# Four plain up-projections at the start of the ConvFFN, its quarter sums made in steps beside them, and the down-projection of a pair one product later

## The chip, the cores and the metric

The kernel runs on one NeuronCore of a Trainium2 chip. The metric is the device time of one execution in microseconds. The engines have the profile's names: PE is the tensor engine (PEld its weight loads), DVE the vector engine (VectorE in the text), ACT the scalar engine (ScalarE), POOL is GpSimd, and SP issues most of the DMAs.

## The reference

A trunk of two layers, d = 1024, over 1024 prompt tokens and 8 x 4 sampled tokens. Each layer is a mixer (RWKV-7, GLA and RetNet heads side by side, then `w_out`), a layer norm, a gated convolutional FFN and another layer norm. The change lies in the FFN alone:

```python
def _conv_ffn(x, conv0, w_up, conv_w, conv_b, w_down):
    t_ = x.shape[1]
    u = x @ w_up                                   # (tokens, 1024) @ (1024, 2 * 2816)
    buf = jnp.concatenate([conv0.astype(u.dtype), u], axis=1)
    c = conv_b + sum(conv_w[j] * buf[:, j:j + t_] for j in range(CONV_W))   # 3 taps over time
    a, b = jnp.split(c, 2, axis=-1)
    return (jax.nn.gelu(a) * b) @ w_down, buf[:, -(CONV_W - 1):]

f, cv = _conv_ffn(x, s_conv[l], ffn_up[l], ffn_conv_w[l], ffn_conv_b[l], ffn_down[l])
x = _layer_norm(ALPHA * x + f, ln2_g[l], ln2_b[l])
```

## The kernel before, in words

Features lie on the 128 partitions, tokens along the free axis in three blocks n = 0, 1, 2 of 384, 384 and 288 columns (`NB`; the last holds the sampled tokens). A matrix product in f32 accuracy is done with operands split into a high and a low half (`split`: ScalarE casts the high half, GpSimd or VectorE subtracts it for the low half), three matmuls for each 128 x 128 weight tile (`mm3`). So x1, the FFN's input, exists as x1h and x1l, eight row tiles (m or k = 0 to 7) for each n; a weight piece of 128 x 512 arrives raw (tag wr, five buffers, `FR`) and becomes wh and wl (six buffers each, `FW`).

The 2816 hidden features are 22 tiles (`NJ`). Tile j has a first half (feature tile j, through the GELU) and a gate half (feature tile j + 22); the two together are called block j here. The blocks are worked in pairs: after the up-projections of a pair come its convolution, gating (`up_gate`, which leaves the gated tile as hh and hl) and, one pair later, its down-projection.

*Plain blocks* (`up_blocks`, blocks 0 and 1): for each n and each of the two feature tiles, two products of 4 k-tiles (12 matmuls each) into a PSUM bank (pu), then bank to u, convolution in c, gating.

*Winograd blocks* (`up`, blocks 2 to 21): for n = 0 and 1 the 2 x 2 block product (two feature tiles or halves of k against two token blocks) is done with seven products instead of eight (pa, pg, pb, pc, pf, pd, pe in the profile). They take sums of weight pieces (s1, s2, s3, s4, made on VectorE from the raw pieces r11, r12, r21, r22) and sums of quarters of x1 (t2, t3, t4, and one that replaces a quarter of x1h and x1l), made once a layer by `sums`. Block n = 2 stays plain beside it (p in the profile), four half products of 12 matmuls with 288 columns.

*The sums before.* At the start of block 1, `residual` adds x1h and x1l into acc for n = 0 and 1 (16 GpSimd instructions a layer). After n = 1 of block 1, `sums` makes the quarter sums from acc, four VectorE instructions for each of four k, each followed by a split.

*The down-projection* (`downs`, `down`): for two halves of the output tiles, two weight pieces (wD) of the pair's two blocks, and for each n and four tiles six matmuls into a bank pd (five buffers, shared with the products), which VectorE adds into acc. `up` of the pair's even block calls it through `between`. The engines' order is set by the framework's scheduler, which knows the order of the code and what each instruction waits for; TensorE follows the code. A tile's buffer is reused when all instructions on the old tile are done.

Of the kernel before, what the change touches and what calls it, by code (L numbers as in the profile page):

```python
# [10 lines left out]
F32 = mybir.dt.float32  # L11
# [158 lines left out]
def step_kernel(ctx: ExitStack, tc: tile.TileContext, xT, wA, wB, wO, wU, wD, pp, pb, lora, bg, bgk, shT, cvT, srw, sgl, srt,  # L170
# [150 lines left out]
    for l in range(depth):  # L321
# [1090 lines left out]
        def wu(t, half):  # L1412
            return wU[l, t, :, 4 * half:4 * half + 4]
# [4 lines left out]
        def whole(ap, name):  # L1418
            return piece(raw_piece(ap, name), name)
# [52 lines left out]

        def residual():

            for k in range(4):
                for n, m in ((0, k), (1, k), (1, k + 4), (0, k + 4)):
                    G.tensor_tensor(acc[n][m], x1[n][0][:, m].bitcast(F32), x1[n][1][:, m].bitcast(F32), ALU.add)

        def sums():


            (h0, l0, _), (h1, l1, _) = x1[:2]
            t2, t3, t4 = ([jp.tile([P, 4, 384], F32R, tag="tq", name=f"{n}{p}", bufs=6) for p in "hl"] for n in ("t2", "t3", "t4"))

            def two(h, lo, raw, e):
                A.copy(h, raw)
                e.tensor_tensor(lo, raw, h.bitcast(F32), ALU.subtract)
            for k in range(4):
                r11, r12, r21, r22 = acc[0][k], acc[1][k], acc[0][k + 4], acc[1][k + 4]
                d1, d2, d3, d4 = (fp.tile([P, 386], F32, tag="u", name="d", bufs=6)[:, 0:384] for _ in range(4))  # L1490
                V.tensor_tensor(d3, r22, r12, ALU.subtract)
                V.tensor_tensor(d1, r12, r11, ALU.subtract)
                V.tensor_tensor(d2, r22, d1, ALU.subtract)
                V.tensor_tensor(d4, r21, d2, ALU.subtract)
                for h, lo, d, e in ((t2[0][:, k], t2[1][:, k], d2, V), (h1[:, k], l1[:, k], d1, V),
                                    (t3[0][:, k], t3[1][:, k], d3, G), (t4[0][:, k], t4[1][:, k], d4, G)):
                    two(h, lo, d, e)
            return [(h0[:, 0:4], l0[:, 0:4]), (h0[:, 4:8], l0[:, 4:8]), (h1[:, 4:8], l1[:, 4:8]), (h1[:, 0:4], l1[:, 0:4]), t2, t3, t4]

# [7 lines left out]

        def up_blocks(j):

            w = [[whole(wu(j + i * NJ, half), f"wU{j}") for half in range(2)] for i in range(2)]  # L1510
            prev, hs, qs = [None] * 2, [], None
            if j:
                residual()
            for n in range(3):
                cs = []
                for i in range(2):
                    t = j + i * NJ
                    ps = bank(n, f"pu{t}")
                    for half in range(2):
                        hf = slice(4 * half, 4 * half + 4)  # L1520
                        product(ps, w[i][half], (x1[n][0][:, hf], x1[n][1][:, hf]), half == 0, half == 1)
                    if n < 2:
                        u = new_u()
                        halo(u, n, prev[i])
                        A.copy(u[:, 2:386], ps)
                        c = conv_prompt(t, i, u, ps, n == 0)
                    else:
                        c, u = conv_samples(t, i, ps)
                        conv_rest(t, c, u, prev[i])
                    prev[i] = u  # L1530
                    cs.append(c)
                hs.append(up_gate(cs, n))
                if n == 0 and j == 0:
                    stats3[0]()
                if n == 1 and j:
                    qs = sums()
            return hs, qs

        def up(j, qs, late=False, between=lambda: None):
# [23 lines left out]
            c11 = conv_prompt(t0, 0, u11, v11, True)  # L1563
            between()
            if not late:
# [10 lines left out]
            v12 = u12[:, 2:386]  # L1576
            V.tensor_tensor(v12, v22, pb_, ALU.add)
            p5 = bank(0, "pc")
            product(p5, piece(s1, "s1"), q1)
# [40 lines left out]
        def down(m, n, group, hs, ws):  # L1620
            ps = pd.tile([P, 512], F32, tag="d", name="pd")[:, :NB[n][1]]
            for i, (h, w) in enumerate(zip(hs, ws)):
                mm3(ps, *w, *h[n], i == 0, i == len(hs) - 1)
            a = acc[n][m]
            if n == 2 and group < 2:

                if group:
                    V.tensor_tensor(a, a, ps, ALU.add)
                V.scalar_tensor_tensor(a, x1[n][group][:, m].bitcast(F32), ALPHA, a if group else ps, ALU.mult, ALU.add)
            elif group:  # L1630
                V.tensor_tensor(a, a, ps, ALU.add)  # L1631
            else:
                V.scalar_tensor_tensor(a, a, ALPHA, ps, ALU.mult, ALU.add)

# [6 lines left out]

        hs, qs = [None] * 2, None
        for j in range(2):
            hs[j], qs = up_blocks(j)
        for j in range(2, NJ - 2, 2):

            a = up(j, qs, between=lambda: downs(j - 2, hs, j // 2 - 1))
            hs = [a, up(j + 1, qs)]

# [215 lines left out]
```

## Time and profile before

| | us |
|---|---|
| median of three runs | 3475.77 (3475.0 to 3477.01) |
| profiled execution | 3467.65 |
| its span, first to last instruction | 3465.5 |
| TensorE busy in it | 3128.6 |
| FFN of the first layer, first to last up-projection pair | about 879 to 1660 from the start |
| FFN of the second layer | about 2616 to 3440 |

In the rows of the profile, a line number is one of the kernel before; L140 stands for all matmuls and L197 for all splits, so the tile names tell them apart. A row of a timeline is start, duration, engine, line, operation, output and inputs, shapes, and in brackets the idle time before it and what ended it. A row of a list of waits is who waited for whom, total us, times, longest. A row of busy time by stretches is start:end and length, busy time and instructions of PE, PEld, DVE, ACT and POOL, the granted clock of TensorE, the DMA share and GB/s.

### The profile page before, as it was taken

The numbers are of one execution on the slowest core, as the hardware profiler recorded it, in microseconds if no ns is written. First come the engines' busy times: TensorE is split into PE (matmuls) and PEld (weight loads), VectorE is DVE, ScalarE is ACT, GpSimd is POOL, SyncE is SP. The second block draws the span as 40 slices with busy tenths as digits, with TensorE's granted clock in tenths as the row PEclk, the third lists the DMA queues.
The fourth block names the chain that finished last, engine by engine and source line by source line (L and its number), as shares of the span: only waits on it lengthen the run. The fifth ranks groups of instructions, "written<-read, shape, count | busy, mean of one in ns | idle before, by whom it ended". The sixth has DMA issues, their size and how long they took to land. (4 is left out here: it accounts for less than half of the span.)

```text
span 3465.5 us, 59055 instructions
## 1 busy us (share of the span) xinstructions
PE 3128.6 (90%) x21570; PEld 2880.9 (83%) x21570; DVE 2382.5 (69%) x5061; ACT 1592.4 (46%) x3639; POOL 1593.6 (46%) x1524
## 2 busy tenths in 40 slices
PE   8889999998799999999788899998987899999995
PEld 8778887778789999999687788876777899998995
DVE  3587764666778776767857667644667786767678
ACT  6653432645443343334585533335555433433346
POOL 5542322145654554545675322121446554555456
PEclk9989999988999999999899899998989999999997
DMA  7443224343211111111364332233432111111111
GB/s 247 144 119 84 75 62 131 113 139 107 52 43 46 43 49 46 40 46 53 97 196 141 107 82 71 64 127 97 140 106 58 46 46 40 49 46 43 44 51 67
DMA packets 245566, 291.14 MB, mean 84 GB/s; under 512 B 76620, under 2 KB 158316, under 8 KB 245276
## 3 DMA queue, kind: packets, MB, share of 16 engines
q1 hardware_dynamic: 225004, 274.08, 25.9%
q10 hardware_dynamic: 20272, 13.29, 1.5%
q8 instruction: 170, 2.79, 0.3%
q14 instruction: 120, 0.98, 0.1%
HBM read 228.85 MB, written 58.43 MB: 83 GB/s over the span
## 5 line engine op out<-in xcount | busy, mean ns | idle before, releaser
L1433 DVE SCALAR_TENSOR_TENSOR c<-u,ppt,c 128x32 f32<-128x32 f32 (+3 forms) x704 | 496.5, 740 | 128.6 <-ACT c L1437 124.3
L197 POOL TENSOR_TENSOR wil<-wir,wih 128x512 fp32r<-128x512 f32 (+1 forms) x264 | 369.0, 1408 | 252.2 <-ACT wih L197 230.1
L140 PE MATMUL gt<-wih,xh 128*128 128x320 f32 (+1 forms) x1008 | 346.4, 345 | 4.6 <-DVE mx L404 4.6
L140 PE MATMUL gt<-wil,xh 128*128 128x320 f32 (+1 forms) x1008 | 321.2, 320 | 4.6 <-POOL wil L197 4.6
L1631 DVE TENSOR_TENSOR acc<-acc,pd 128x384 f32<-128x384 f32 (+1 forms) x464 | 230.7, 516 | 99.3 <-PE pd L140 99.1
L140 PE MATMUL gt<-wih,xl 128*128 128x320 f32 x896 | 285.3, 318 | 0.0
L197 ACT CAST wih<-wir 128x512 fp32r<-128x512 f32 (+1 forms) x296 | 185.1, 637 | 138.7 <-PE po L140 61.9
L140 PE MATMUL pa<-xh,wih 128*128 128x384 f32 (+1 forms) x576 | 208.1, 361 | 29.1 <-ACT wih L197 11.3
L653 DVE TENSOR_TENSOR tm<-U,N 96x60 f32<-96x60 f32 (+24 forms) x558 | 173.3, 310 | 78.0 <-DMA N<-gd 62.9
L140 PEld LDWEIGHTS gt<-wih,xh 128*128 128x128 f32 (+1 forms) x1008 | 191.7, 190 | 42.0 <-issue 24.5
L140 PE MATMUL pa<-xh,wil 128*128 128x384 f32 (+1 forms) x576 | 196.4, 341 | 12.9 <-POOL wil L197 11.6
L140 PEld LDWEIGHTS gt<-wil,xh 128*128 128x128 f32 (+1 forms) x1008 | 192.9, 191 | 8.4 <-POOL wil L197 6.9
L140 PE MATMUL pa<-xl,wih 128*128 128x384 f32 (+1 forms) x576 | 195.1, 339 | 1.2 <-POOL xl L197 1.2
L655 DVE TENSOR_TENSOR U<-U,tm 96x60 f32<-96x60 f32 (+24 forms) x558 | 170.1, 305 | 16.3 <-DMA ydram<-ys 0.4
L140 PEld LDWEIGHTS gt<-wih,xl 128*128 128x128 f32 x896 | 176.2, 197 | 0.0
L197 POOL TENSOR_TENSOR hl<-c,hh 128x384 fp32r<-128x384 f32 x132 | 147.3, 1127 | 55.6 <-ACT hh L197 55.6
L140 PEld LDWEIGHTS pa<-xh,wih 128*128 128x128 f32 x576 | 116.6, 202 | 43.6 <-ACT wih L197 12.6
L1437 ACT ACTIVATE c<-u,ppt 128x384 f32<-128x384 f32 x160 | 113.1, 708 | 74.2 <-POOL hl L197 38.2
L140 PE MATMUL po<-yh,wih 128*128 128x384 f32 (+1 forms) x384 | 138.5, 361 | 8.6 <-DVE ac L1349 7.6
L140 PE MATMUL po<-yh,wil 128*128 128x384 f32 (+1 forms) x384 | 130.6, 340 | 2.2 <-DVE wil L197 2.2
L140 PEld LDWEIGHTS pa<-xh,wil 128*128 128x128 f32 x576 | 116.5, 202 | 17.3 <-POOL wil L197 15.8
L140 PE MATMUL po<-yl,wih 128*128 128x384 f32 (+1 forms) x384 | 130.4, 339 | 0.0
(958 smaller groups left out, 10257.4 us busy)
## 6 DMA issues: line engine op xcount, KB each, us to landing
wir<-in_wA_dram SPq DMA_DIRECT2D x144, 256.0 KB
wir<-in_wO_dram SPq DMA_DIRECT2D x96, 256.0 KB
wir<-in_wB_dram SPq DMA_DIRECT2D x56, 320.0 KB
tokd<-ev SPq DMA_DIRECT2D x112, 160.0 KB
x<-rkvd SPq DMA_DIRECT2D x16, 576.0 KB
tk<-tokd SPq DMA_DIRECT2D x16, 480.0 KB
rkvd<-mx SPq DMA_DIRECT2D x36, 192.0 KB
tk<-tokd SPq DMA_DIRECT2D x16, 400.0 KB
```

The costliest lines, as they stand in the source:

```text
L140: self.order(self.engine.matmul(out, lhsT, rhs, start=start, stop=stop), cols, 4 if rhs.dtype == F32 else 1)
L197: return A.copy(dst_h, src), (le or G).tensor_tensor(dst_l, src, dst_h.bitcast(F32), ALU.subtract)
L653: V.tensor_tensor(tm, U[:, 0:nr, i:i + 1].to_broadcast([4 * ns, nr, 31 - i]), N[:, i:i + 1, i + 1:32].to_broadcast([4 * ns, nr, 31 - i]), ...
L655: V.tensor_tensor(U[:, 0:nr, i + 1:32], U[:, 0:nr, i + 1:32], tm, ALU.add)
L1433: V.scalar_tensor_tensor(cv[..., o:], uu[..., tap + o:tap + w], pc(PP_CV + 4 * t + tap), cv[..., o:], ALU.mult, ALU.add)
L1437: A.activation(c, src, AF.Identity, scale=pc(PP_CV + 4 * t + 2), bias=pc(PP_CV + 4 * t + 3))
L1631: V.tensor_tensor(a, a, ps, ALU.add)
```

## The change

Blocks 2 and 3 become plain too (`up_first` for block 0, `up_plain` for blocks 1 to 3, which work through one feature tile and its three n before the other). `residual` is gone: the accumulation of the first pair adds x1h and x1l itself, in two VectorE instructions for every tile. `sums` becomes a generator in five steps, called by `then` after given points of blocks 1 to 3, and works from x1h and x1l instead of acc; the last step replaces the quarter of x1. In a Winograd block `between` stands behind the sum of product pb instead of in front of the second half product of n = 2.

```diff
-        def residual():
-
-            for k in range(4):
-                for n, m in ((0, k), (1, k), (1, k + 4), (0, k + 4)):
-                    G.tensor_tensor(acc[n][m], x1[n][0][:, m].bitcast(F32), x1[n][1][:, m].bitcast(F32), ALU.add)
...
+            def apart(e, a, b):
+
+                d, f = new(), new()
+                e.tensor_tensor(d, a[0], b[0], ALU.subtract)
+                e.tensor_tensor(f, a[1], b[1], ALU.subtract)
+                e.tensor_tensor(d, d, f, ALU.add)
+                return d
+
+            def minus(e, a, d):
+
+                e.tensor_tensor(d, a[0], d, ALU.subtract)
+                e.tensor_tensor(d, d, a[1], ALU.add)
             for k in range(4):
-                r11, r12, r21, r22 = acc[0][k], acc[1][k], acc[0][k + 4], acc[1][k + 4]
...
-                V.tensor_tensor(d3, r22, r12, ALU.subtract)
-                V.tensor_tensor(d1, r12, r11, ALU.subtract)
-                V.tensor_tensor(d2, r22, d1, ALU.subtract)
-                V.tensor_tensor(d4, r21, d2, ALU.subtract)
...
+                d = apart(G, x(1, k + 4), x(1, k))
+                two(t3[0][:, k], t3[1][:, k], d, G)
+                d = apart(V, x(1, k), x(0, k))
+                minus(V, x(1, k + 4), d)
+                two(t2[0][:, k], t2[1][:, k], d, G)
+                f = new()
+                V.tensor_tensor(f, x(0, k + 4)[0], d, ALU.subtract)
+                V.tensor_tensor(f, f, x(0, k + 4)[1], ALU.add)
+                two(t4[0][:, k], t4[1][:, k], f, V)
+                yield
+            for k in range(4):
+                d = apart(V if k % 2 else G, x(1, k), x(0, k))
+                two(h1[:, k], l1[:, k], d, V)
+            yield
...
+        def up_plain(j, between, then):
+
+            hs, cs = [], []
+            for i in range(2):
+                t = j + i * NJ
+                w, prev = [whole(wu(t, half), f"wU{t}") for half in range(2)], None
+                for n in range(3):
+                    c, prev = plain(t, i, n, w, prev)
+                    cs.append(c)
+                    if i:
+                        hs.append(up_gate((cs[n], c), n))
+                    then(j, i, n)
+                if i == 0:
+                    between()
+            return hs
...
             c11 = conv_prompt(t0, 0, u11, v11, True)
-            between()
             if not late:
                 product(p1, piece(r21, "a21"), x2[0], True, False)
...
             V.tensor_tensor(v12, v22, pb_, ALU.add)
+            between()
             p5 = bank(0, "pc")
...
-            if n == 2 and group < 2:
-
-                if group:
-                    V.tensor_tensor(a, a, ps, ALU.add)
-                V.scalar_tensor_tensor(a, x1[n][group][:, m].bitcast(F32), ALPHA, a if group else ps, ALU.mult, ALU.add)
-            elif group:
+            if group:
                 V.tensor_tensor(a, a, ps, ALU.add)
             else:
-                V.scalar_tensor_tensor(a, a, ALPHA, ps, ALU.mult, ALU.add)
+
+                for x, y in zip(x1[n][:2], (ps, a)):
+                    V.scalar_tensor_tensor(a, x[:, m].bitcast(F32), ALPHA, y, ALU.mult, ALU.add)
...
-        hs, qs = [None] * 2, None
-        for j in range(2):
-            hs[j], qs = up_blocks(j)
-        for j in range(2, NJ - 2, 2):
-
-            a = up(j, qs, between=lambda: downs(j - 2, hs, j // 2 - 1))
-            hs = [a, up(j + 1, qs)]
+
+        make = sums()
+        qs = next(make)
+        times = ((1, 0, 2), (1, 1, 2), (2, 0, 2), (2, 1, 2), (3, 1, 1))
+
+        def then(*at):
+            if at in times:
+                next(make)
+        hs = []
+        for j in range(0, NJ - 2, 2):
+
+            def between():
+                if j:
+                    downs(j - 2, hs, j // 2 - 1)
+            if j == 0:
+                a = up_first()
+            elif j < 4:
+                a = up_plain(j, between, then)
+            else:
+                a = up(j, qs, between=between)
+            hs = [a, up(j + 1, qs) if j >= 4 else up_plain(j + 1, lambda: None, then)]
```

Where instructions stand now. First GpSimd around the down-projection of blocks 4 and 5 (wD4, wD5), which stands in block 6 (its weights are wU6 and wU28, its splits a21 and s2; hl are the low halves of the gated tiles of block 5). Before:

```order
L197 TENSOR_TENSOR wD4wl<-wD4r,wD4wh 128x512
L197 TENSOR_TENSOR wD5wl<-wD5r,wD5wh 128x512
L1454 COPY cvt<-u 128x16
L1453 COPY cvt<-u 128x2
L197 TENSOR_TENSOR wD4wl<-wD4r,wD4wh 128x512
L197 TENSOR_TENSOR hl<-c,hh 128x384
L197 TENSOR_TENSOR wD5wl<-wD5r,wD5wh 128x512
L197 TENSOR_TENSOR a21wl<-wU28r,a21wh 128x512
L1454 COPY cvt<-u 128x16
L1453 COPY cvt<-u 128x2
L197 TENSOR_TENSOR hl<-c,hh 128x384
L197 TENSOR_TENSOR hl<-c,hh 128x288
```

The same place in the changed kernel:

```order
L197 TENSOR_TENSOR a21wl<-wU28r,a21wh 128x512
L197 TENSOR_TENSOR s2wl<-wU6r,s2wh 128x512
L1454 COPY cvt<-u 128x16
L1453 COPY cvt<-u 128x2
L197 TENSOR_TENSOR wD4wl<-wD4r,wD4wh 128x512
L197 TENSOR_TENSOR hl<-c,hh 128x384
L197 TENSOR_TENSOR wD5wl<-wD5r,wD5wh 128x512
L1454 COPY cvt<-u 128x16
L1453 COPY cvt<-u 128x2
L197 TENSOR_TENSOR hl<-c,hh 128x288
L197 TENSOR_TENSOR hl<-c,hh 128x384
L197 TENSOR_TENSOR wD4wl<-wD4r,wD4wh 128x512
```

The splits of a21 and s2 moved ahead of all wD splits; the gated tiles' halves stand behind the first two wD splits instead of four, and that of n = 2 comes before that of n = 1.

VectorE's sums of weights for block 6 (s1, then wU28 for r21, wU6 for r11 and r12). Before, they stand beside the first accumulations of the down-projection, behind the sum of pg:

```order
L1569 TENSOR_TENSOR s1r<-wU28r 128x512
L1433 SCALAR_TENSOR_TENSOR c<-u,ppt,c 128x32
L1562 TENSOR_TENSOR u<-u,pg 128x384
L1433 SCALAR_TENSOR_TENSOR c<-u,ppt,c 128x32
L1570 TENSOR_TENSOR wU28r<-wU6r,wU28r 128x512
L1631 TENSOR_TENSOR acc_10128<-acc_10128,pd 128x384
L1571 TENSOR_TENSOR wU6r<-s1r,wU6r 128x512
L1433 SCALAR_TENSOR_TENSOR c<-u,ppt,c 128x383
L1631 TENSOR_TENSOR acc_10129<-acc_10129,pd 128x384
L1572 TENSOR_TENSOR wU6r<-wU6r 128x512
```

In the changed kernel, they stand between the sums of products pb, pf, pc and pd of block 5:

```order
L1602 TENSOR_TENSOR s1r<-wU28r 128x512
L1610 TENSOR_TENSOR u<-u,pb 128x384
L1603 TENSOR_TENSOR wU28r<-wU6r,wU28r 128x512
L1616 TENSOR_TENSOR u<-u,pf 128x384
L1604 TENSOR_TENSOR wU6r<-s1r,wU6r 128x512
L1617 TENSOR_TENSOR u<-u,pc 128x384
L1605 TENSOR_TENSOR wU6r<-wU6r 128x512
L1623 TENSOR_TENSOR u<-u,pd 128x384
```

They moved forward by about a block's second half, past the convolution and gating of block 5.

GpSimd at block 1 (wU1 are its weights; acc the residual sums). Before, these rows are the end of a run of 15 sums between two weight splits:

```order
L1477 TENSOR_TENSOR acc_10131<-x1h_9172,x1l_9173 128x384
L1477 TENSOR_TENSOR acc_10139<-x1h_9682,x1l_9683 128x384
L1477 TENSOR_TENSOR acc_10143<-x1h_9682,x1l_9683 128x384
L197 TENSOR_TENSOR wU1wl<-wU1r,wU1wh 128x512
L1477 TENSOR_TENSOR acc_10135<-x1h_9172,x1l_9173 128x384
```

In the changed kernel (d are the temporaries of the quarter sums):

```order
L197 TENSOR_TENSOR wU23wl<-wU23r,wU23wh 128x512 x2
L1453 COPY cvt<-u 128x2
L197 TENSOR_TENSOR wU2wl<-wU2r,wU2wh 128x512 x2
L1454 COPY cvt<-u 128x16 x2
L1453 COPY cvt<-u 128x2
L197 TENSOR_TENSOR hl<-c,hh 128x384
L1495 TENSOR_TENSOR d<-x1h_9682 128x384
L1496 TENSOR_TENSOR d<-x1l_9683 128x384
```

No sum stands ahead of a split of block 1's weights any more.

More of the change, by code (lines that the diff above doesn't have):

```diff
@@ L1483, in sums, with x, new @@
             t2, t3, t4 = ([jp.tile([P, 4, 384], F32R, tag="tq", name=f"{n}{p}", bufs=6) for p in "hl"] for n in ("t2", "t3", "t4"))
+            def x(n, k):
+                return [t[:, k].bitcast(F32) for t in x1[n][:2]]
+            qs = [(h0[:, 0:4], l0[:, 0:4]), (h0[:, 4:8], l0[:, 4:8]), (h1[:, 4:8], l1[:, 4:8]), (h1[:, 0:4], l1[:, 0:4]), t2, t3, t4]
+            yield qs
+            def new():
+                return fp.tile([P, 386], F32, tag="u", name="d", bufs=6)[:, 0:384]
             def two(h, lo, raw, e):
@@ L1487, in two @@
                 e.tensor_tensor(lo, raw, h.bitcast(F32), ALU.subtract)
-            for k in range(4):
-                r11, r12, r21, r22 = acc[0][k], acc[1][k], acc[0][k + 4], acc[1][k + 4]
-                d1, d2, d3, d4 = (fp.tile([P, 386], F32, tag="u", name="d", bufs=6)[:, 0:384] for _ in range(4))
-                V.tensor_tensor(d3, r22, r12, ALU.subtract)
-                V.tensor_tensor(d1, r12, r11, ALU.subtract)
-                V.tensor_tensor(d2, r22, d1, ALU.subtract)
-                V.tensor_tensor(d4, r21, d2, ALU.subtract)
[L1495 to L1498, printed above, removed]
+            def apart(e, a, b):
[7 more added lines that the diff above has]
+                e.tensor_tensor(d, d, a[1], ALU.add)
+            for k in range(4):
+                d = apart(G, x(1, k + 4), x(1, k))
[12 more added lines that the diff above has]
+            yield
         def product(ps, w, x, first=True, last=True):
@@ L1506, in bank, with plain, up_first @@
             return (pg.tile([P, 512], F32, tag="g", name=name) if n == 2 else pd.tile([P, 512], F32, tag="d", name=name))[:, :NB[n][1]]
[L1508 to L1513, printed above, removed]
+        def plain(t, i, n, w, prev):
+            ps = bank(n, f"pu{t}")
+            for half in range(2):
+                hf = slice(4 * half, 4 * half + 4)
+                product(ps, w[half], (x1[n][0][:, hf], x1[n][1][:, hf]), half == 0, half == 1)
+            if n < 2:
+                u = new_u()
+                halo(u, n, prev)
+                A.copy(u[:, 2:386], ps)
+                return conv_prompt(t, i, u, ps, n == 0), u
+            c, u = conv_samples(t, i, ps)
+            conv_rest(t, c, u, prev)
+            return c, u
+        def up_first():
+            w = [[whole(wu(i * NJ, half), "wU") for half in range(2)] for i in range(2)]
+            prev, hs = [None] * 2, []
             for n in range(3):
@@ L1516, in up_blocks @@
                 for i in range(2):
[L1517 to L1530, printed above, removed]
+                    c, prev[i] = plain(i * NJ, i, n, w[i], prev[i])
                     cs.append(c)
                 hs.append(up_gate(cs, n))
-                if n == 0 and j == 0:
+                if n == 0:
                     stats3[0]()
-                if n == 1 and j:
-                    qs = sums()
-            return hs, qs
+            return hs
[12 more added lines that the diff above has]
+                    between()
+            return hs
         def up(j, qs, late=False, between=lambda: None):
```

## The prediction

> **What bounds the kernel now.** I read the page's engine table first, then busy time by stretches, TensorE's list of waits, and the timelines of TensorE, ScalarE and GpSimd around one wait.
>
> ```profile
> PE 3128.6 (90%) x21570; PEld 2880.9 (83%) x21570; DVE 2382.5 (69%) x5061; ACT 1592.4 (46%) x3639; POOL 1593.6 (46%) x1524
> ```
>
> TensorE (PE) is the bound, so the change is priced in TensorE time. The stretches of one pair of Winograd blocks (start:end, length, then each engine's busy time, granted clock):
>
> ```profile
> 1100.12:1107.40 7.28, 5.37 (x29) 4.80 (x28) 7.14 (x11) 4.58 (x11) 5.24 (x6) 1.00 0.11 36
> 1107.40:1112.00 4.60, 4.18 (x14) 3.53 (x14) 4.60 (x8) 1.25 (x3) 2.72 (x3) 0.63 0.01 4
> 1112.00:1128.45 16.45, 16.05 (x105) 15.88 (x103) 10.79 (x23) 2.00 (x4) 2.54 (x2) 1.00 0.16 48
> 1128.45:1170.41 41.96, 41.96 (x266) 41.96 (x265) 29.18 (x46) 19.85 (x50) 25.52 (x25) 1.00 0.16 51
> ```
>
> The up-projection products (last row) run without a gap at full clock, 41.96 us for two blocks. The down-projection (first three) loses time at its start, and behind the gap the granted clock is 0.63. TensorE's waits in the two layers (total us, times, longest):
>
> ```profile
> PE pd L140 <- POOL hl L197: 20.9, 11, 2.1
> PE pd L140 <- DVE acc L1631: 5.7, 12, 1.2
> PE pd L140 <- POOL hl L197: 20.0, 10, 2.1
> PE pd L140 <- DVE acc L1631: 7.2, 15, 0.8
> ```
>
> One wait of 2.1 us per pair, always on the low half of a gated tile (hl), then a short one on the accumulation. Matmul starts show cadence and cost:
>
> ```profile
> 908.70 0.29 PE L140 MATMUL pu<-x1l,wU0wh 128*128 128x288 f32 x1
> 908.83 0.30 PE L140 MATMUL pu<-x1h,wU0wl 128*128 128x288 f32 x1
> 908.97 0.34 PE L140 MATMUL pu<-x1h,wU1wh 128*128 128x384 f32 x1
> 909.14 0.34 PE L140 MATMUL pu<-x1l,wU1wh 128*128 128x384 f32 x1
> 1107.59 0.56 PE L140 MATMUL pd<-hl,wD5wh 128*128 128x384 f32 x1 [2.09 <-POOL hl L197]
> ```
>
> Starts are 0.133 us apart at 288 columns and 0.174 at 384 (168 and 96 of them make the 41.96 us; the rows are rounded). A down-projection has 96 of 384 and 48 of 288: 16.7 + 6.4 = **23.1 us**. What the 18 down-projections inside Winograd pairs take (first, last, and the line under the 18):
>
> ```profile
> 1028.62:1058.16 29.54, 26.69 (x146) 25.58 (x145) 27.18 (x45) 7.91 (x17) 10.06 (x10) 0.88 0.12 36
> 3331.19:3359.80 28.61, 25.83 (x145) 24.53 (x145) 22.66 (x39) 7.85 (x17) 10.61 (x10) 0.94 0.12 38
> sum 519.23, PE 462.67 PEld 436.80 DVE 419.68 ACT 143.49 POOL 194.37; mean PE 25.70 PEld 24.27 DVE 23.32 ACT 7.97 POOL 10.80
> ```
>
> 519.2 - 18 x 23.1 = **103.4 us** lost there. Why hl is late:
>
> ```profile
> 1087.87 0.62 ACT L197 CAST wD4wh<-wD4r 128x512 fp32r<-128x512 f32 x1 [0.61 <-DMA wD4r<-in_wD_dram]
> 1092.52 0.62 ACT L197 CAST wD5wh<-wD5r 128x512 fp32r<-128x512 f32 x1 [4.03 <-DMA wD5r<-in_wD_dram]
> 1097.15 0.62 ACT L197 CAST wD4wh<-wD4r 128x512 fp32r<-128x512 f32 x1 [2.27 <-DMA wD4r<-in_wD_dram]
> 1101.78 0.62 ACT L197 CAST wD5wh<-wD5r 128x512 fp32r<-128x512 f32 x1
> ...
> 1082.84 1.32 POOL L197 TENSOR_TENSOR s4wl<-wU5r,s4wh 128x512 fp32r<-128x512 f32 x1
> 1088.65 1.28 POOL L197 TENSOR_TENSOR wD4wl<-wD4r,wD4wh 128x512 fp32r<-128x512 f32 x1
> 1099.15 1.34 POOL L197 TENSOR_TENSOR hl<-c,hh 128x384 fp32r<-128x384 f32 x1
> 1102.53 1.51 POOL L197 TENSOR_TENSOR wD5wl<-wD5r,wD5wh 128x512 fp32r<-128x512 f32 x1 [2.04 <-PE pd L140]
> 1104.00 1.60 POOL L197 TENSOR_TENSOR a21wl<-wU28r,a21wh 128x512 fp32r<-128x512 f32 x1
> 1106.52 2.32 POOL L197 TENSOR_TENSOR hl<-c,hh 128x384 fp32r<-128x384 f32 x2
> ```
>
> The four wD pieces come 4.6 us apart: four of the five raw buffers are held by the block's own weights, so they pass one after another through the fifth. ScalarE stands 4.03 and 2.27 us on these loads, with the convolution queued behind; on GpSimd the late hl stands behind wD5 and a21.
>
> The other losses are in the first blocks, from the second plain up-projection to the second pair, in layers 1 and 2:
>
> ```profile
> 908.97:1021.29 112.32, 93.04 (x554) 92.48 (x553) 87.61 (x128) 46.55 (x116) 72.19 (x69) 0.91 0.11 35
> 2646.44:2758.55 112.11, 92.79 (x554) 92.24 (x553) 87.51 (x128) 47.05 (x115) 71.57 (x69) 0.91 0.12 36
> PE pu L140 <- POOL wU1wl L197: 10.4, 1, 10.4
> PE pg L140 <- ACT c L1437: 8.9, 1, 8.9
> ```
>
> The first wait is a weight split behind 15 residual sums on GpSimd, the second a bank that ScalarE frees late, held up by the Winograd sums. Neither is the price of needed work.
>
> **The change part by part.** *Plain blocks 2 and 3.* Each Winograd block replaces 8 products by 7, so two plain ones add 2 x 12 matmuls a layer: 24 x 0.174 = 4.2 us a layer. A plain block is 96 x 0.174 + 48 x 0.133 = 23.1 us.
>
> *Residual and sums.* The 32 GpSimd sums vanish with the wait of 10.4 us. The quarter sums, 42 VectorE and 26 GpSimd instructions a layer, go beside three plain blocks (69 us), and the first Winograd down-projection that needs the last of them is 11 us into block 4. The bank wait of 8.9 us loses its cause. In the accumulation of the first down-projection every tile now takes two VectorE instructions instead of one:
>
> ```profile
> L1629 DVE SCALAR_TENSOR_TENSOR acc<-x1h,pd x16: 440/453/455, 974.0 to 2724.1; 128x288 f32<-128x288 f32 x16
> L1629 DVE SCALAR_TENSOR_TENSOR acc<-x1l,acc x16: 457/853/1557, 1044.9 to 2796.4; 128x288 f32<-128x288 f32 x16
> L1633 DVE SCALAR_TENSOR_TENSOR acc<-acc,pd x32: 540/554/555, 964.8 to 2720.9; 128x384 f32<-128x384 f32 x32
> L1477 POOL TENSOR_TENSOR acc<-x1h,x1l x32: 985/1322/1361, 906.1 to 2661.6; 128x384 f32<-128x384 f32 x32
> ```
>
> The second kind runs from 0.457 to 1.557 us; scaled by 384/288 its least is 0.61 and its median 1.14. VectorE then needs 16 x (0.55 + 0.61) + 8 x (0.45 + 0.46) = 25.8 us at least, 16 x 1.69 + 8 x 1.30 = 37.4 at the median, against TensorE's 23.1. GpSimd has about 12 instructions of 1.3 us in that stretch, half of it, so I take the middle, **32 us**. [...]
>
> Sum for this region: 3 x 23.1 + 32 = 101.3 against 112.3 and 112.1: **-11.0 and -10.8, together -21.8 us**, the extra products included. The up-projection of block 0 before it is unchanged.
>
> *Down-projection one product later.* The half product with a21 (12 x 0.133 = 1.6 us) and the one with s2 (12 x 0.174 = 2.1) now run first: it starts 3.7 us later against an hl that is 2.1 us late. That holds even if hl comes no earlier; behind it now stands the n = 2 half first (about 1 us), which leaves 0.6. It should come earlier: GpSimd does hl before the second pair of wD splits, with a21 long done. What is late next? A wD piece now needs the raw buffer that the s2 split frees. s4's split of the block before ends at 1082.84 + 1.32 = 1084.2; that frees the buffer for s1. VectorE computes s1, r21, r11 between its sums, r11 behind the sum of product pf:
>
> ```profile
> 1087.22 0.56 DVE L1582 TENSOR_TENSOR u<-u,pf 128x384 f32<-128x384 f32 x1 [0.62 <-PE pf L140]
> ```
>
> So r11 is done about 1089, s2's halves (0.6 + 1.3) by 1091. A load takes from 1088.65 + 1.28 to 1092.52, 2.6 us. The first wD piece is ready about 1095.5, the second 4.6 later at 1100.1, the third 1104.7, the fourth 1109.3. TensorE wants the first at 1100.12 + 3.7 = 1103.8, the second 0.5 later, the others 11.5 later: slack of 4 us. I cost s2's weights at nothing for the same reason: wanted at 1101.7. The loads are as many as before, and SP issues those of a pair in the same order. Queued behind VectorE's new early s1 are sums of pb and pf, with a later user. The bank of pb is now one of the five that the down-projection turns, at its fifth tile, 4 x 1.04 us in; the sum that frees it is one instruction of 0.55 us.
>
> If the wait goes, its clock goes: gain 103.4. For the first pair of each layer I take no gain, since the last step of the sums (six GpSimd, ten VectorE instructions) falls on its start: 103.4 - 6.4 - 5.5 = **91.5 us**.
>
> **Sum.** 91.5 + 21.8 = 113.3. The profiled execution took 3467.65 (span 3465.5), the median of the runs 3475.77, 0.23% more: 3354.4 by the one, **3362.5 by the other; I predict 3363**. All of it gone and 25.8 in the first down-projection: 103.4 + 34.2 = 137.6, 3338.
>
> **Rivals.**
> 1. *Half the wait stays*: wD or hl comes later than worked out, a gap of a microsecond and its slow matmuls remain. For it: the second wD piece has 4 us only, and GpSimd's hl stands behind it. Gain 46 + 22: 3408.
> 2. *The slow stretch isn't the gap's.* The waits make 20.9 + 5.7 + 20.0 + 7.2 = 54 us, half of the 103; the rest is slow matmuls at a granted clock of 0.63. If they would come anyway, the gain is 54 + 22: 3400. Against: no slow matmul in the gapless products. [...]
> 3. *The later place moves the wait along*: hl and TensorE shift together, only the first region gains: 3454.
> 4. *Slower*: the one raw buffer. If s2's split ends only as TensorE starts its product, the first wD piece comes 4.6 us later and the second 9.2: waits of 2.5 and 4.1 us and 2.7 of slow matmuls, 9.3 a pair instead of 5.7: +65 - 22 = +43, 3519. Waiting begins where s2's split ends less than 2 x 4.6 - 0.5 = 8.7 us before the down-projection. It decides where the loss is 5.7 + 21.8 / 18 = 6.9 us a pair, a wait of 4.2: at a split 4.5 us before. Against: 1091 is 13 us before.
>
> **How the numbers follow.** Forecast 0.70; rival 1 0.13; 2 0.04; 3 0.05; 4 0.08, a quarter of which ends near no change. The range 3335 to 3425 holds the forecast, nearly, and the first two rivals. 0.2% (7 us) is about what a measurement tells from nothing: faster 0.92, same 0.02, slower 0.06.
>
> **What the profile after would show.** Down-projections of 23 to 24 us at clock 1.00 and no wait on hl; no row for wU1wl or pg among TensorE's long waits; the first down-projection near 32 us with waits on the accumulation; 48 more matmuls. I am wrong if TensorE waits for wD or s2 in each pair, or if the first down-projection exceeds 40 us.

## The result and the profile after

The changed kernel took **3390.55 us** (median of four runs, 3384.56 to 3395.68) beside 3476.39 of the kernel before: ratio 0.9744, 95% interval 0.9711 to 0.9776. Measured again beside later runs, it took 3399.35 beside 3469.29: 0.9800 (0.9780 to 0.9820). The prediction was 3363, with a range of 3335 to 3425: the sign and the range hold, the gain is about three quarters of the forecast 113 us in the first measurement (85.8) and six tenths in the second (69.9). The profiled execution took 3395.68, 72.0 us less than that of before.

TensorE's row of the page, which answers to the first row of the prediction:

```profile
PE 3103.4 (91%) x21618; PEld 2868.3 (85%) x21618; DVE 2374.4 (70%) x5085; ACT 1577.6 (46%) x3635; POOL 1575.1 (46%) x1512
```

48 matmuls more, as worked out, and still 25 us less busy time, since the slow matmuls of the down-projections inside the Winograd pairs are gone (462.67 us busy in these 18 before, 423.89 now). What lies outside the FFN took from 1820 to 1844 us in the profiled executions of this study, in no order that an edit explains, so I use the two FFN stretches, from the first up-projection's first matmul to the end of the last down-projection. (In the kernel before, the second layer's last up-projection ends at 3394.6 and its FFN at 3431.1; the table ahead has about 3440.) Busy time by stretches, of before:

```profile
878.80:1695.79 816.99, 760.79 (x4520) 743.92 (x4520) 607.19 (x974) 334.15 (x790) 445.27 (x418) 0.96 0.15 44
2616.33:3431.08 814.75, 758.18 (x4521) 741.54 (x4522) 606.33 (x974) 335.14 (x792) 447.38 (x418) 0.96 0.15 44
```

and of after:

```profile
883.26:1661.35 778.09, 745.55 (x4544) 734.78 (x4544) 605.00 (x986) 327.67 (x790) 438.53 (x412) 0.98 0.16 47
2579.99:3358.67 778.68, 746.09 (x4545) 736.22 (x4546) 604.13 (x986) 327.33 (x788) 438.28 (x412) 0.98 0.16 46
```

Together 1631.7 before and 1556.8 after: **-75.0 us**. Three places make it up. The first is the 18 down-projections inside the Winograd pairs (first, second, the worst, last, and the line under the 18):

```profile
1038.24:1061.60 23.36, 23.36 (x145) 23.36 (x145) 14.80 (x30) 4.94 (x10) 7.95 (x9) 1.00 0.23 68
1103.55:1128.00 24.45, 23.58 (x145) 23.05 (x145) 16.56 (x31) 5.79 (x13) 11.29 (x11) 1.00 0.21 65
...
1502.28:1527.75 25.47, 23.45 (x145) 22.93 (x145) 17.64 (x31) 5.77 (x13) 10.85 (x11) 1.00 0.21 62
...
3267.71:3292.13 24.42, 23.50 (x145) 23.00 (x145) 16.95 (x32) 5.75 (x12) 10.79 (x11) 1.00 0.22 66
sum 439.64, PE 423.89 PEld 414.83 DVE 295.84 ACT 103.71 POOL 195.25; mean PE 23.55 PEld 23.05 DVE 16.44 ACT 5.76 POOL 10.85
```

519.2 before, 439.6 now, **-79.6**; the clock is 1.00 in all. The second is the region from the first up-projection to block 4, the third block 4 with its down-projection (first and third row: the first layer):

```profile
883.26:1019.85 136.59, 125.32 (x724) 121.28 (x725) 112.03 (x169) 60.31 (x150) 82.42 (x77) 0.93 0.16 40
2579.99:2717.95 137.96, 125.74 (x724) 122.11 (x725) 112.81 (x169) 60.48 (x150) 82.73 (x77) 0.92 0.17 40
1019.85:1071.55 51.70, 46.33 (x278) 46.01 (x277) 37.20 (x59) 17.03 (x42) 28.96 (x26) 0.93 0.14 42
2717.95:2770.28 52.33, 46.95 (x278) 46.63 (x277) 37.23 (x59) 17.02 (x42) 28.97 (x26) 0.93 0.14 41
```

The region took 142.5 and 142.2 before (the starts are 878.80 to 1021.29 and 2616.33 to 2758.55): **-10.2** in the two layers together. Block 4 took 50.5 and 49.6 with a down-projection of 29.5 and 28.6 in it, and now 51.7 and 52.3 with one of 23.4 and 23.2: its products lost 7.4 and 8.2 us, **+15.6**. The three make -74.2.

The largest of TensorE's waits that are left in the FFN ahead of its last pair, over both layers (who for whom, total us, times, longest):

```profile
PE pd L140 <- DVE u L1610: 15.3, 16, 2.0
PE pd L140 <- ACT c L1437: 11.9, 4, 4.6
PE p L140 <- ACT c L1437: 10.7, 2, 5.4
PE pd L140 <- DVE acc L1664: 8.3, 2, 4.2
```

The rows on hl, wU1wl and pg that the prediction showed are no longer among the long waits. New are pb's bank (L1610, in 16 of 18 pairs), the waits of the first down-projection (ACT c and acc), and p1's bank in block 4 (p).

### The profile page after: what moved, and what is told of

Same layout as the page of the kernel before. It is cut to its first block, busy times and chain, and to the rows that moved or that the text cites. A ratio compares the mean times of both kernels' runs of the same rounds, so it can differ in the third digit from the quotient of the medians.

```text
span 3393.9 us, 59056 instructions
## 1 busy us (share of the span) xinstructions
PE 3103.4 (91%) x21618; PEld 2868.3 (85%) x21618; DVE 2374.4 (70%) x5085; ACT 1577.6 (46%) x3635; POOL 1575.1 (46%) x1512
## 5 line engine op out<-in xcount | busy, mean ns | idle before, releaser
L1433 DVE SCALAR_TENSOR_TENSOR c<-u,ppt,c 128x32 f32<-128x32 f32 (+3 forms) x704 | 514.2, 762 | 71.3 <-ACT c L1437 65.9
L1660 DVE TENSOR_TENSOR acc<-acc,pd 128x384 f32<-128x384 f32 (+1 forms) x480 | 239.4, 517 | 112.7 <-PE pd L140 110.2
L140 PEld LDWEIGHTS gt<-wil,xh 128*128 128x128 f32 (+1 forms) x1008 | 193.6, 192 | 10.1 <-POOL wil L197 8.6
L197 POOL TENSOR_TENSOR hl<-c,hh 128x384 fp32r<-128x384 f32 x132 | 139.4, 1066 | 53.0 <-ACT hh L197 53.0
L140 PE MATMUL po<-yh,wih 128*128 128x384 f32 (+1 forms) x384 | 136.1, 354 | 12.1 <-DVE ac L1349 10.2
L1437 ACT ACTIVATE c<-u,ppt 128x384 f32<-128x384 f32 x144 | 101.8, 708 | 85.3 <-DVE u L1633 39.9
```

The source lines that it names most:

```text
L140: self.order(self.engine.matmul(out, lhsT, rhs, start=start, stop=stop), cols, 4 if rhs.dtype == F32 else 1)
L197: return A.copy(dst_h, src), (le or G).tensor_tensor(dst_l, src, dst_h.bitcast(F32), ALU.subtract)
L1433: V.scalar_tensor_tensor(cv[..., o:], uu[..., tap + o:tap + w], pc(PP_CV + 4 * t + tap), cv[..., o:], ALU.mult, ALU.add)
L1437: A.activation(c, src, AF.Identity, scale=pc(PP_CV + 4 * t + 2), bias=pc(PP_CV + 4 * t + 3))
```

## The experiments

| | us | ratio to before, 95% | both FFN stretches |
|---|---|---|---|
| changed kernel, first | 3390.55 | 0.9744 (0.9711 to 0.9776) | 1556.8 |
| e8 changed kernel again, beside e5 to e7 | 3399.35 | 0.9800 (0.9780 to 0.9820) | 1565.2 |
| e1 move only | 3409.16 | 0.9826 (0.9801 to 0.9851) | 1565.6 |
| e2 plain blocks only | 3464.47 | 0.9987 (0.9968 to 1.0006) | 1630.1 |
| e3 sum first | 3370.52 | 0.9713 (0.9688 to 0.9738) | 1534.7 |
| e4 last step later | 3403.07 | 0.9805 (0.9777 to 0.9833) | 1570.6 |
| e5 residual spread | 3399.46 | 0.9793 (0.9769 to 0.9817) | 1558.1 |
| e6 no sums | 3353.27 | 0.9661 (0.9635 to 0.9687) | 1523.4 |
| e7 last step in block 4 | 3390.75 | 0.9779 (0.9757 to 0.9802) | 1552.4 |
| e9 steps off the first down-projection | 3402.20 | 0.9801 (0.9767 to 0.9835) | 1566.5 |
| e10 sums on VectorE | 3370.41 | 0.9718 (0.9679 to 0.9757) | 1532.6 |
| e11 e3 and e7 | 3354.75 | 0.9668 (0.9634 to 0.9703) | 1524.4 |
| e12 e3 and e10 | 3343.62 | 0.9634 (0.9613 to 0.9655) | 1508.9 |

Each ratio is to the kernel before, run beside it on the same chip. The FFN stretches come from one profile each.

**The changed kernel once more (e8)**, without an edit.

> The changed kernel once more, unchanged, beside these runs on one chip, so that the edits can be compared with it and not only with the kernel before: 0.9744 of the kernel before by the first measurement, its FFN parts from the first up-projection to the last down-projection 778.1 and 778.7 us.

It came out at 0.9800, and its FFN parts at 784.6 and 780.6 us, 8.4 more together; the last section shows why.

**Which half of the change brings the gain (e1, e2).** The one keeps everything of before but the call's place, the other the change without it.

```diff
             c11 = conv_prompt(t0, 0, u11, v11, True)
-            between()
...
             V.tensor_tensor(v12, v22, pb_, ALU.add)
+            between()
```

> The kernel before with the call of between() moved behind pb's sum and nothing else changed. Theory A (the gain is that of the 18 down-projections of the Winograd pairs, and needs nothing of the other part): 3476 - 80 = 3396 us (3390 to 3402), the 18 down-projections at 24.4 us each but two, no wait on hl, and the wait on pb's bank of 0.9 us in 16 of them. Theory B (the new order of the first blocks is what brings half of it): 3425 to 3440 us. The first region stays at 142 us either way.

> The changed kernel with between() put back to its old place, ahead of block j's s2 product in the Winograd pairs; four plain up-projections first and stepwise sums stay. Theory A: the wait on hl of 2.1 us is back in all 18 down-projections, which take 28.8 us each; the first region gains 5 us a layer and block 4 loses it again waiting for p1's bank, so 3465 to 3480 us, no difference from before to 0.3%. Theory B: the first blocks alone bring 22 to 45 us, 3430 to 3455.

The move alone shortens the FFN by 66 us, the plain blocks and stepwise sums alone by 1.7, nothing that the ratio can tell. In e2 the old waits are back, in the words of the kernel before:

```profile
PE pd L140 <- POOL hl L197: 36.1, 19, 2.1
PE pd L140 <- DVE acc L1660: 32.1, 26, 6.2
```

Theory A of e2 holds in 16 of the 18 pairs. In the first pair of each layer there is no wait on hl; block 4 gives most of the region's gain back, as A says (53.9 and 54.3 us), but waiting 6.2 us for acc and not for p1's bank. In e1 theory A holds for the pairs: 18 of them, block and down-projection together, give 74.5 us. But A's 80 us were too many, and the first region, which was to stay at 142 us, took 145.4 and 148.0: the first Winograd pair, which needs the sums there, loses 2.9 and 7.0. The two halves make 68 us apart and 75 together; the 7 between were not taken apart. The move brings most of the gain.

**The new wait on pb's bank (e3).** VectorE, ScalarE and TensorE around it, in the changed kernel (start, duration, engine, line, and in brackets the idle time before):

```profile
1105.80 0.54 DVE L1596 TENSOR_TENSOR u<-u,pg 128x384 f32<-128x384 f32 x1
1107.18 1.27 DVE L1433 SCALAR_TENSOR_TENSOR c<-u,ppt,c 128x383 f32<-128x383 f32 x2 [0.84 <-ACT c L1437]
1108.36 0.55 DVE L1610 TENSOR_TENSOR u<-u,pb 128x384 f32<-128x384 f32 x1
...
1106.44 0.71 ACT L1437 ACTIVATE c<-u,ppt 128x384 f32<-128x384 f32 x1 [1.04 <-DVE u L1596]
...
1108.97 0.45 PE L140 MATMUL pd<-hh,wD4wh 128*128 128x384 f32 x1 [0.87 <-DVE u L1610]
```

VectorE has summed pg by 1106.34, then stands idle for 0.84 us until ScalarE has done the start of c11 (to 1107.15), does c11's two taps (the two convolution steps on VectorE), and only then the sum of pb, 0.55 us, that frees the bank. pb's last matmul ends at 1103.72, just as the down-projection starts (1103.55). So the price isn't the sum's 0.55 us but the queue ahead of it. e3 puts both taps behind the sum, by a dependency on it:

```diff
-            c11 = conv_prompt(t0, 0, u11, v11, True)
+            c11 = conv_start(t0, 0, v11, 384)
...
-            V.tensor_tensor(v12, v22, pb_, ALU.add)
+            summed = V.tensor_tensor(v12, v22, pb_, ALU.add)
+            taps(t0, c11, u11[:, 0:386], c11, 384, True, summed)
             between()
```

> The changed kernel with c11's two taps on VectorE put behind pb's sum by a dependency. Theory A (the 0.9 us wait on pb's bank is VectorE held up by these taps, which wait for ScalarE): the wait falls below 0.2 us, the down-projections go from 24.45 to 23.2 us, and 16 times 1.2 us are gained: 3390 - 19 = 3371 us, ratio to before 0.969. Rival (the wait is VectorE being late for another reason, or the time is lost again at c11's conv, whose gating feeds hh): 3390 us, ratio 0.974, with the wait under another name.

VectorE's rows of e3 at the same place:

```profile
1106.07 0.54 DVE L1596 TENSOR_TENSOR u<-u,pg 128x384 f32<-128x384 f32 x1
1106.54 0.54 DVE L1610 TENSOR_TENSOR u<-u,pb 128x384 f32<-128x384 f32 x1
1107.45 0.62 DVE L1433 SCALAR_TENSOR_TENSOR c<-u,ppt,c 128x383 f32<-128x383 f32 x1 [0.37 <-ACT c L1437]
```

The wait is gone from TensorE's list, and the down-projections take what their columns need (a stretch of e3):

```profile
1104.58:1127.77 23.19, 23.19 (x145) 23.19 (x145) 16.34 (x31) 5.45 (x11) 10.08 (x11) 1.00 0.21 69
```

The FFN falls by 22.1 us, 22.0 of it in the 16 pairs, 1.37 each; the forecast was 19. (Beside the second profile of the changed kernel, in which more pairs wait 2.0 us, it falls by some 30.) Not all of it is the bank. In the changed kernel TensorE is also held for the second wD piece: GpSimd's split of it ends 0.84 to 1.16 us after the down-projection's start, and its first matmul is the sixth, at 5 x 0.174 = 0.87. In the pair shown, the split ends at 1104.43, and these two matmuls start 0.22 and 0.29 us after the one ahead of each, instead of 0.174 (the first of them follows one at 1104.26):

```profile
1104.48 0.44 PE L140 MATMUL pd<-hh,wD5wl 128*128 128x384 f32 x1
1104.77 0.34 PE L140 MATMUL pd<-hh,wD4wh 128*128 128x384 f32 x1
```

By the starts of the matmuls this costs 0.10 to 0.45 us a pair, and the wait on the bank about 1.15 (2.3 in one pair): some 3 and 19 us of the 22. In e3 the split ends between 0.11 us ahead of the start and 0.48 after it, and neither the hold nor the wait on the bank is left; why the split comes earlier there was not followed. That the taps held up the bank, theory A, is shown.

**Block 4 (e4, e7).** In the changed kernel TensorE waits there for ScalarE's use of p1's bank (the product pu of block 3, n = 2), and ScalarE for the last step's sums:

```profile
1031.30 0.51 ACT L1489 CAST x1h<-d 128x384 fp32r<-128x384 f32 x1 [2.45 <-DVE d L1497]
...
1032.06 0.61 ACT L1437 ACTIVATE c<-pu,ppt 128x288 f32<-128x288 f32 x1
...
1032.72 0.61 PE L140 MATMUL p<-x1h,a21wh 128*128 128x288 f32 x1 [5.37 <-ACT c L1437]
```

e4 makes the last step one product later, e7 in block 4 just ahead of its down-projection.

```diff
e4  -(2, 1, 2), (3, 1, 1))      +(2, 1, 2), (3, 1, 2))
e7  -(2, 1, 2), (3, 1, 1))      +(2, 1, 2))
e7  +                if j == 4:
e7  +                    next(make)
                     if j:
                         downs(j - 2, hs, j // 2 - 1)
```

> The changed kernel with the last step of the sums made one product later, after (3,1,2) in place of (3,1,1). Theory A (the 5.4 us wait of block 4's p on p1's bank is ScalarE's casts of x1h, which wait for VectorE's and GpSimd's sums and stand ahead of the copies that free the bank): the wait falls from 5.4 to 2 us or less, and with the slow matmuls behind it 4 to 7 us a layer are gained: 3377 to 3383 us, ratio 0.971 to 0.973. Rival (ScalarE is late by its own work in block 3, whatever the casts): the wait stays at 4 to 5.5 us, ratio 0.974.

> The changed kernel with the last step of the sums moved out of block 3 into block 4, ahead of the down-projection there. Theory A (block 4 loses about 6 us because the last step stands ahead of the work that frees p1's bank, and its own down-projection has room for it): block 4 with its down-projection falls from 51.7 and 52.3 us to 46 to 47, 10 to 12 us in both layers, ratio 0.971. Rival (as with the step one product later, the work only delays the next thing in line, here VectorE's sums that free the banks of the down-projection): 50 to 54 us, ratio 0.974 to 0.976.

e4 removed the wait on p1's bank and got nothing for it: block 4 took 54.0 and 51.1 us. TensorE's waits in the first layer's:

```profile
PE pd L140 <- ACT wD3wh L197: 2.8, 1, 2.8
PE pd L140 <- DVE u L1610: 2.4, 1, 2.4
PE pd L140 <- POOL wD3wl L197: 0.9, 1, 0.9
```

The cause that A named is right and its gain wrong: the same step now holds up ScalarE's cast of wD3. e7 takes the work past that too, and block 4 falls to 46.6 and 46.8, from 50.9 and 52.2 in the changed kernel's profile beside it; no wait above 0.6 us is left in it.

The ratio (0.9779 beside 0.9800) doesn't separate e7 from the changed kernel by itself; the stretches do.

**The first down-projection (e5, e9).** It took 37.7 and 39.2 us, and all of the waits on ACT c and on acc L1664 in the list of after are its own (5.5 and 4.2 us in the first layer). e5 moves 20 of the 24 second residual instructions to later groups; e9 moves two steps of the sums.

```diff
e5  +            replaced = n == 1 and m < 4
e5  +            if not group:
e5  +                V.scalar_tensor_tensor(a, x1[n][0][:, m].bitcast(F32), ALPHA, ps, ALU.mult, ALU.add)
e5  +            if group == (0 if replaced else 1 + m % 4):
e5  +                V.scalar_tensor_tensor(a, x1[n][1][:, m].bitcast(F32), ALPHA, a, ALU.mult, ALU.add)
e9  -(2, 0, 2), (2, 1, 2), (3, 1, 1))      +(2, 1, 1), (3, 0, 1), (3, 1, 1))
```

> The changed kernel with VectorE's second instruction of the residual (the x1l part) left in group 0 only for the four tiles that the sums replace (n = 1, m below 4), and for the other 20 spread over groups 1 to 4, five in each. Theory A (the end of the first down-projection is paced by VectorE's two instructions for each bank): the 4.2 us wait on acc goes, and the first down-projection falls from 37.7 and 39.2 us by 4 to 6 us each, the later ones stay at 24.4 to 24.6: 8 to 12 us in all, ratio 0.971. Rival (ScalarE and VectorE are late there by the sums of x1 alone): it stays above 36 us, ratio 0.974.

> The changed kernel with the third and fourth step of the sums moved from (2,0,2) and (2,1,2), the first of which stands right ahead of the first down-projection, to (2,1,1) and (3,0,1). Theory A (the waits of 3.7, 1.8 and 4.2 us in the first down-projection are ScalarE's and VectorE's queues held up by these steps): they fall below 3 us together, the region from 136.6 and 138.0 us to 130 to 132, about 12 us in both layers, ratio 0.977 where the changed kernel had 0.980 on this chip and 0.974 on the other. Rival (the work of the sums is the same and only waits elsewhere): the region stays at 135 to 139 us with the waits under pu.

In e5 the waits of the first layer's stand unchanged, under the new line number:

```profile
PE pd L140 <- ACT c L1437: 5.5, 2, 3.7
PE pd L140 <- DVE acc L1663: 4.2, 1, 4.2
```

The first down-projection took 38.1 and 39.0: theory A of e5 has fallen. (Block 4 took 49.8 and 50.2, its wait on p1's bank 3.9 and 4.2: what little e5 gave, it gave there.) In e9 the region fell by 2.5 and 3.5 us (134.1 and 134.5; down-projection 35.1 and 35.6), but block 4 took 56.5 and 56.6, with waits of 9.8 and 10.1 us on p1's bank: the work of the sums was moved, and its wait with it.

**What the sums cost (e6, e10).** e6 leaves the sums out; e10 gives GpSimd's share of them to VectorE.

```diff
e6  -            t2, t3, t4 = ([jp.tile([P, 4, 384], F32R, tag="tq", name=f"{n}{p}", bufs=6) for p in "hl"] for n in ("t2", "t3", "t4"))
e6  +            t2, t3, t4 = ((h0[:, 0:4], l0[:, 0:4]) for _ in range(3))
...
e6  -            for k in range(4):
e6  -                d = apart(G, x(1, k + 4), x(1, k))
...
e6  +            for _ in range(5):
                 yield
...
e10 -                d = apart(G, x(1, k + 4), x(1, k))
e10 -                two(t3[0][:, k], t3[1][:, k], d, G)
e10 +                d = apart(V, x(1, k + 4), x(1, k))
e10 +                two(t3[0][:, k], t3[1][:, k], d, V)
...
e10 -                two(t2[0][:, k], t2[1][:, k], d, G)
e10 +                two(t2[0][:, k], t2[1][:, k], d, V)
...
e10 -                d = apart(V if k % 2 else G, x(1, k), x(0, k))
e10 +                d = apart(V, x(1, k), x(0, k))
```

> The changed kernel with the sums of x1 left out altogether: the Winograd pairs read quarters of x1 in their place (the output is not the reference's), everything else stays. It prices the stepwise sums. Theory A (the sums beside the plain blocks cost what ScalarE, VectorE and GpSimd lose in the first down-projection and at block 4): the region falls from 136.6 to 130 to 132 us, block 4 with its down-projection from 51.7 to 45.5 to 47, so 22 to 26 us in both layers, about 3366 us. Theory B (the sums are hidden and the first down-projection is slow by its own two instructions for each bank): the region stays above 134 us, block 4 near 50, 3380 us or more.

> The changed kernel with all of the sums' additions on VectorE, those of GpSimd too. In the region VectorE's 128x384 additions took 0.55 us at best and 1.0 to 1.65 us where GpSimd worked beside them. Theory A (GpSimd's part slows VectorE by as much as it takes off it): five more additions of 0.55 us in each of four steps are paid by shorter ones, and the region stays within 4 us of 136.6 and 138.0. Rival (GpSimd's help is real): VectorE has 5 x 0.55 = 2.8 us a step more to do, the waits grow, and the region takes 140 to 150 us.

e6: the region of the first layer, block 4 with its down-projection, and the first down-projection:

```profile
885.78:1007.96 122.18, 120.57 (x724) 118.69 (x725) 81.58 (x140) 58.05 (x144) 54.52 (x58) 0.97 0.18 47
...
1007.96:1052.07 44.11, 44.11 (x279) 44.11 (x277) 25.33 (x46) 13.27 (x32) 18.49 (x19) 1.00 0.14 42
950.19:973.48 23.29, 23.29 (x146) 23.22 (x145) 21.89 (x45) 3.76 (x9) 5.24 (x6) 1.00 0.14 46
```

Theory B is refuted. The sums cost 14.4 and 15.6 us in the region and 7.6 and 8.2 in block 4, more than twice what A expected of the region: 46 us in the two layers, although all their instructions lie beside TensorE's. (The FFN as a whole shows 33 of them, since more pairs than in the first profile lost the race told of at the end.) And the first down-projection, still with two instructions for each tile, runs in 23.3 us with no wait: VectorE is busy for 21.9 us of it, and at least three of the 48 instructions that the tiles take come behind it (45 fall in it), without TensorE being held up.

e10: the region, block 4 and the first down-projection, in the first layer (131.5, 45.6 and 32.6 in the second):

```profile
877.06:1008.22 131.16, 123.86 (x724) 121.04 (x725) 110.72 (x195) 61.50 (x153) 61.30 (x56) 0.95 0.17 43
1008.22:1053.32 45.10, 44.41 (x278) 44.09 (x277) 33.28 (x60) 16.13 (x41) 22.80 (x20) 1.00 0.14 43
941.58:973.74 32.16, 26.47 (x146) 25.46 (x145) 32.16 (x64) 8.13 (x19) 8.32 (x7) 0.89 0.10 33
```

VectorE executes 26 instructions more in the region (195 against 169) and is busy for less time, 110.7 us against 112.0. The rival is refuted, and theory A too small: without GpSimd's help the FFN is 24 us shorter. One group as an example, in the changed kernel and in e10 (mean ns of one behind the busy time):

```profile
L1503 DVE TENSOR_TENSOR d<-d,x1l 128x384 f32<-128x384 f32 x4 | 5.4, 1357 | 0.1
```

```profile
L1503 DVE TENSOR_TENSOR d<-d,x1l 128x384 f32<-128x384 f32 x4 | 3.3, 813 | 0.0
```

e10 also takes away a chain of three GpSimd instructions of 1.2 us ahead of each cast of t3h, where VectorE's of that size took 0.54 to 0.56 us in the changed kernel at their shortest; how much of the 24 us is that and how much the shorter VectorE instructions was not separated.

**Together (e11, e12).** The edits of e3 and e7, and of e3 and e10.

> The two edits that shortened their place together: c11's taps behind pb's sum, and the last step of the sums in block 4. If they add: 22 us of the first and 10 us of the second, the FFN parts from 778.1 and 778.7 us to 761 and 763, ratio 0.970 beside 0.980 of the changed kernel on the same chip. Rival (with the taps later, block 4's down-projection has no room for the sums): block 4 back above 49 us, ratio 0.973.

> c11's taps behind pb's sum, and all of the sums' additions on VectorE, together. If they add: the region at 131.2 and 131.5 us as with the second alone, the down-projections of the Winograd pairs at 23.2 us as with the first, the FFN parts from 778.1 and 778.7 us to 756 and 754, about 3345 us, ratio 0.964. Rival (VectorE with all sums has no room for the taps' new place in block 4, or the region gives back): FFN parts above 762 us, no better than the taps with the last step in block 4 (0.967).

Both add up: 1524.4 and 1508.9 us of FFN against 1524 and 1510 expected. e12 is the fastest kernel of the study, 0.9634 of before. Its region takes 131.2 and 132.0 us, and block 4 in the first layer:

```profile
1012.14:1056.31 44.17, 44.17 (x278) 44.17 (x277) 33.08 (x59) 15.96 (x40) 22.77 (x20) 1.00 0.13 44
```

From block 4 on next to nothing is lost in the pairs; the 9 us of the first layer's region over e6's 122.2 are the first down-projection, 32.3 us.

## Why the prediction was right, and where it was not

*The wait on hl and its slow clock.* Right in that both vanished together in all 18 pairs, and e2 brought the wait back in 16. Rival 2 (the slow stretch comes anyway) and rival 3 (the wait moves along) are refuted. Rival 1 came half true under another name: a wait of 0.9 us stayed in most pairs, on pb's bank and at clock 1.00. But the slow clock alone did not set the price, as "if the wait goes, its clock goes" suggests. Before the change, it stayed at 1.00 behind the same gap of 2.1 us in two of the 18 pairs, and these took about as long as the others (28.3 to 30.5):

```profile
2906.72:2935.19 28.47, 24.52 (x145) 23.00 (x145) 22.64 (x39) 7.92 (x17) 10.53 (x10) 1.00 0.13 38
3190.09:3218.36 28.27, 24.45 (x146) 22.98 (x145) 22.47 (x39) 7.86 (x17) 10.41 (x10) 1.00 0.12 38
```

There TensorE waited 1.8 and 1.7 us for accumulations, instead of the 0.6 of the pair that the prediction shows: between them VectorE had the weight sums of the next block, which the change moved forward as well. How the gain divides between the earlier hl and VectorE's freer queue, no run separates.

*The bank of pb.* The mis-sized term. It was costed at nothing because "the sum that frees it is one instruction of 0.55 us"; VectorE's queue ahead of that instruction was not looked at. Together with the second wD piece it measured 1.37 us in each of 16 pairs, 22.0 by e3, some 19 of them the bank's.

*The first pair of each layer.* Taken as no gain; its down-projections took 23.4 and 23.2, nearly the full gain, 11.6 of 11.9 us in both. But the last step's sums, which were to fall on them, fell a few microseconds earlier, on block 4's product p: 15.6 us that the sum didn't hold. Together the term was wrong by 4.0, each half by more.

*The first down-projection.* 32 us taken, 37.4 as the top; 37.7 and 39.2 measured. No run shows the 32, the author's middle of two estimates: in the changed kernel the 48 instructions on the tiles took 28.4 and 29.8 us of VectorE. The step that failed is the mechanism: VectorE's pace on the tiles (e5 refutes it; e6 runs them in 23.3 with the same instructions). What counts is what VectorE and ScalarE still owe to the sums when it starts. "The bank wait of 8.9 us loses its cause" fails with it: the sums hold banks up as before, now pd's. The region gained 10.2 and not 21.8.

*The slack of 4 us of the wD pieces.* Wrong: the second piece had none, and the price was small. r21 is overwritten by VectorE only after a21's split, which the chain left out:

```profile
1090.58 0.69 DVE L1603 TENSOR_TENSOR wU28r<-wU6r,wU28r 128x512 f32<-128x512 f32 x1 [2.76 <-POOL a21wl L197]
```

```profile
1093.18 1.37 POOL L197 TENSOR_TENSOR s2wl<-wU6r,s2wh 128x512 fp32r<-128x512 f32 x1 [2.64 <-issue]
...
1102.87 1.56 POOL L197 TENSOR_TENSOR wD5wl<-wD5r,wD5wh 128x512 fp32r<-128x512 f32 x1 [2.35 <-ACT u L1451]
```

s2's split ends at 1094.55, not 1091: 9 us before the down-projection's start at 1103.55, near the 8.7 at which rival 4 begins to wait. The second piece's split ends at 1104.43, just where TensorE wants it. So the prediction's own sign of being wrong, a wait for wD in each pair, is there in small, some 3 us in all; only in two pairs is it long enough for the list of waits (0.16 and 0.17 us). No run changed the number of raw buffers, so rival 4's price was not tried.

The sum: the 16 later pairs gained 68.0 and not 91.5 (23.5 less), the first pairs 11.6 that were not counted, the region 10.2 and not 21.8 (11.6 less), and 15.6 in block 4 were not foreseen: 113.3 - 23.5 + 11.6 - 11.6 - 15.6 = 74.2, where the stretches give 75.0. That the medians differ by 85.8, nearer to the forecast, is luck: the median of before lies 8.7 us above its profiled execution, that of the changed kernel 5.1 below. (In the prediction's sentence on the starts of matmuls, the 168 are those of 384 columns and the 96 those of 288; its sums use them so.)

## What to carry to other kernels

When something new waits for the instruction that frees a bank, price not that instruction's own duration but its engine's queue up to it, from the last instruction known to be done, waits included. Work "beside" the bound engine was not free where the instructions behind it in its queues could not wait: here 46 us of the sums showed up as waits for banks and slower matmuls behind them, and moving them (e4, e9) moved the waits, while putting them where what stands behind them could wait (e7, 9.7 us in block 4), or all on one engine (e10, 24 us of the FFN), paid. Sharing additions between VectorE and GpSimd cost more than it saved here (e10); try one engine alone.

## What was not expected of the hardware

A GpSimd subtraction and the second of VectorE's two taps held one another up (VectorE by 1.1 us or GpSimd by 0.45), in a race for which went first. In the changed kernel's second profile, two pairs have the same starts to the hundredth, 0.70 and 0.71 us apart; first VectorE's rows of both, then GpSimd's:

```profile
1101.27 2.38 DVE L1433 SCALAR_TENSOR_TENSOR c<-u,ppt,c 128x383 f32<-128x383 f32 x2 [0.84 <-ACT c L1437]
1170.34 1.27 DVE L1433 SCALAR_TENSOR_TENSOR c<-u,ppt,c 128x383 f32<-128x383 f32 x2 [0.84 <-ACT c L1437]
```

```profile
1101.97 1.26 POOL L197 TENSOR_TENSOR wD4wl<-wD4r,wD4wh 128x512 fp32r<-128x512 f32 x1 [1.08 <-ACT wD4wh L197]
1171.05 1.71 POOL L197 TENSOR_TENSOR wD6wl<-wD6r,wD6wh 128x512 fp32r<-128x512 f32 x1 [1.08 <-ACT wD6wh L197]
```

In the one GpSimd takes 1.26 us and the taps run 1.1 us longer than in the other, where GpSimd takes 0.45 longer. The record of the second tap starts 48 ns ahead of GpSimd's in the one and 50 ns in the other. The same can be compared in all nine profiles in which the down-projection stands behind pb's sum and the taps ahead of it (the changed kernel twice, e1, e4 to e7, e9, e10), in 120 pairs where GpSimd starts within 0.2 us of the tap. With at most 46 ns between the starts VectorE is held in all 20 pairs, at 47 to 49 ns in 18 of 49, from 50 ns on in none of 51. So a few nanoseconds decide between equal shapes here; why VectorE is held although its record starts first, no row shows. The order decides 25.5 us against 24.4 for a down-projection, because TensorE's wait behind the taps is 2.0 us instead of 0.9, and 27.0 to 27.4 where the granted clock falls as well. VectorE lost the race in one pair of 16 in the changed kernel's first profile and in six in the second, which is most of the 8.4 us between the two; in e3, e11 and e12, where the taps stand behind the sum, TensorE doesn't wait for it in any pair.

After a wait of 2.0 us the granted clock dropped in some pairs and not in others: in 16 of the 38 pairs of these nine profiles in which VectorE is held. Two of the second profile:

```profile
1097.64:1124.77 27.13, 25.16 (x146) 24.62 (x145) 17.67 (x31) 5.80 (x13) 10.83 (x11) 0.94 0.20 59
...
1233.12:1258.68 25.56, 23.54 (x145) 23.00 (x145) 17.67 (x31) 5.79 (x13) 10.85 (x11) 1.00 0.19 62
```

After waits of 0.9 us it never did (1.00 in all 15 such pairs of the first profile). Why equal gaps of 2.0 us end differently, no run shows.
